# Seven half products for eight in the first SwiGLU too, some low parts by accumulating loads, and one conditioning vector moved to the second SwiGLU

## The chip, the cores and the metric

The kernel runs on one core of one Trainium2 chip. The metric is device time of one execution in microseconds. The kernel before takes 1032.04 us, the median of three runs between 1031.98 and 1033.32 us. Differences of about 0.2%, some 2 us, can be told from no change.

## What is computed

One decoder layer on 512 tokens of width 1024, in float32:

```python
def _swiglu(h, w_gate, w_up, w_down):
    return (jax.nn.silu(h @ w_gate) * (h @ w_up)) @ w_down
...
c_act = jax.nn.silu(c)
mod = (c_act @ w_ada[l] + b_ada[l]).reshape(B, N_MOD, D_MODEL)[:, :, None, :]
sh1, sc1, gt1, sh2, sc2, gt2, sh3, sc3, gt3 = [mod[:, i] for i in range(N_MOD)]
h = _modulate(_rmsnorm(x, g_ffn1[l]), sh1, sc1)
x = x + MACARON_W * gt1 * _swiglu(h, w1_gate[l], w1_up[l], w1_down[l])
h = _modulate(_rmsnorm(x, g_mix[l]), sh2, sc2)
x = x + gt2 * _hybrid_mixer(h, ...)
h = _modulate(_rmsnorm(x, g_ffn2[l]), sh3, sc3)
x = x + MACARON_W * gt3 * _swiglu(h, w2_gate[l], w2_up[l], w2_down[l])
return _rmsnorm(x, g_final)
```

The hidden width of both SwiGLUs is 2816, that is 22 blocks of 128. The mixer between them (a convolution and an attention branch) has the same code before and after. The nine vectors of `mod` condition the three parts; vector 8 is `gt3`, the gate of the second SwiGLU.

## The kernel before

**Precision.** Every float32 operand of a product is split in a high part (rounded to float32r) and a low part (the rest), and a product is three matmuls: high by high, low by high, high by low. For weights, a unit of 128x1024 values is loaded by SP into one of four buffers `raw`; ScalarE copies it to `whi` (L496); VectorE, or now and then GpSimd, subtracts and writes `wlo` (L435, `low_part`). There are four pairs `whi`, `wlo`, so a unit is split three or four units ahead of its use.

**Stages.** The first SwiGLU (`ffn`, from about 60 to 407 us of the trace), the mixer (to about 640 us) and the second SwiGLU (`ffn2`, to the end). In `ffn` each of the blocks 3 to 21 is a pair of full products, gate and up (`project`): 2 x 8 x 2 x 3 = 96 matmuls of 256 columns. The down products come in two halves of 11 blocks (`part`), each added to the residual `x`. While it runs, VectorE also multiplies and sums seven conditioning vectors (`ada_sums`, L1242 and L1245, eight instructions each, with their own loads into three buffers `araw`), and builds the rotary tables.

**Seven for eight.** In `ffn2`, from block `PLAIN` = 7 on, the gate and up products of a block are made of seven half products in place of eight (`seven`): 7 x 4 x 3 = 84 matmuls. For that VectorE builds sums of the activations once (`build_t`: `thi`, `tlo`, L819 to L829), sums of the two weight units for each block (`sums`, L461 to L472) with their own high and low parts (`sum_parts`: `wsh`, `wsl`, L479 and L481), and adds the half products up (`collect`, L901 to L922). Two of these adds are waited for by later products of the same block: the product after L908 adds into its bank, and the one after L914 into another. The down products of `ffn2` come in four groups (`SIZES` = 6, 6, 5, 5).

**What sets the order.** A planner (`Plan`) runs the tasks of the program against cost estimates and writes each engine's instructions in one fixed order. For an elementwise step that VectorE or GpSimd can do, it picks one of them; GpSimd is charged with `W_TAX` on top.

Of the kernel before, what the change touches and what calls it, by code (L numbers as in the profile page):

```python
# [25 lines left out]
FH = FK // 2  # L26
# [4 lines left out]
PLAIN = 7  # L31
# [65 lines left out]
N_AW = 3  # L97
LATER, ADA_FROM = 3, 2
# [17 lines left out]
R_T = 0.9  # L116
# [177 lines left out]
def tile_hymba_layer(ctx: ExitStack, tc: tile.TileContext, xT, pos, cols_d, con_d, wa0, wa1, f1a, f1b, f1d,  # L294
# [62 lines left out]
    def ffn_units(wa, wb, wd):  # L357
        u = [wa[d] for d in range(DK)]
        u += [wb[f - GRP, i] for f in range(GRP, FH) for i in range(2)]
        u += [wd[0, n] for n in range(FH)]  # L360
        u += [wb[f - GRP, i] for f in range(FH, FK) for i in range(2)]
        return u + [wd[1, n] for n in range(FH)]

# [15 lines left out]
    def seven_units(wa, wb, wd, at):  # L379
# [22 lines left out]
    units += seven_units(f2a, f2b, f2d, len(units))  # L402
# [29 lines left out]
    def low_part(u):  # L432
# [4 lines left out]
        if u not in pair_of or u != pair_of[u].u:  # L437
            give(raws, i)
        done(made[u])
# [45 lines left out]
    def make_units():  # L485
        for u in range(len(units)):
# [13 lines left out]
            go(R_W, low_part(u))  # L500
# [209 lines left out]
    def ffn(s, gp, accs, norm, end):  # L710
        ghi = [gp.tile([P, T], F32R, name=f"ghi{k}") for k in range(FH)]
        glo = [gp.tile([P, T], F32R, name=f"glo{k}") for k in range(FH)]
        sg_of = [gp.tile([P, T], F32, name=f"sg{k}") for k in range(2)]
        lag(64, gp)
        for k in range(KEEP[s]):
            whi_of.append(gp.tile([P, UNIT], F32R, name=f"whik{k}"))
            wlo_of.append(gp.tile([P, UNIT], F32R, name=f"wlok{k}"))
            give(kept[s], len(whi_of) - 1)
        sgs, gs = Slots(range(2)), [Slots([k]) for k in range(FH)]
        g_in = [Event() for _ in range(FK)]  # L720
        gate = [mod[:, 3 * s + 2, d:d + 1] for d in range(DK)]
        at = {}

        def glu(f, bg, bu):
            k = yield sgs
            yield c_act(T)
            nc.scalar.activation(sg_of[k], bank_of[bg], AF.Silu)
            give(banks, bg)
            q = yield scr
            yield c_tt(T)  # L730
            nc.vector.tensor_mul(scr_of[q], sg_of[k], bank_of[bu])  # L731
            give(banks, bu)
            give(sgs, k)
            j = yield gs[f % FH]
            yield c_act(T)
            nc.scalar.activation(ghi[j], scr_of[q], AF.Copy)
            yield c_tt(T)
            nc.vector.tensor_sub(glo[j], scr_of[q], ghi[j].bitcast(F32))
            give(scr, q)
            done(g_in[f])  # L740

        def part(half, d, b, ts, keep=False):
            for k in range(FH):
                n = d * FH + k
                if (half, n // 8) not in at:
                    at[half, n // 8] = take_unit()
                u = at[half, n // 8]
                yield made[u]
                yield g_in[half * FH + k]
                yield c_mm3(ts.stop - ts.start)  # L750
                mm3(bank_of[b][:, ts], cols(u, n % 8), (ghi[k][:, ts], glo[k][:, ts]), k == 0, k == FH - 1)
                if n % 8 == 7 and not keep:
                    free_unit(u)
                if half == 0 and d == DK - 1:
                    give(gs[k], k)

        def first_half(d, b):
            yield c_stt(T)
            nc.vector.scalar_tensor_tensor(x[d], bank_of[b], gate[d], x[d], op0=OP.mult, op1=OP.add)
            give(banks, b)  # L760

        def main():
            for f in range(GRP):
                go(R_GLU, glu(f, accs[2 * f], accs[2 * f + 1]))
            for f in range(GRP, FK):
                if f == FH:
                    for d in range(DK):
                        b = yield banks
                        yield from part(0, d, b, FULL)
                        if d == 0:  # L770
                            yield mod_in[3 * s + 2]
                        go(R_X, first_half(d, b))
                bg = yield banks
                yield from project(bg, N_THIRDS if f == GRP else 0)
                bu = yield banks
                yield from project(bu)
                go(R_GLU, glu(f, bg, bu))
            for d in range(DK - 2):
                b = yield banks
                yield from part(1, d, b, FULL)  # L780
                go(R_X, residual(d, b, gate[d], FULL, norm))
# [5 lines left out]
            for n in range(8, FH):  # L787
                free_unit(at[1, n])
# [1508 lines left out]
```

## Time and profile before

| | before |
|---|---|
| median of 3 runs | 1032.04 us |
| the profiled execution | 1032.0 us |
| its span | 1030.2 us |
| TensorE (PE) busy | 1001.6 us, 97% |
| VectorE (DVE) busy | 723.5 us, 70% |
| ScalarE (ACT) busy | 449.6 us, 44% |
| GpSimd (POOL) busy | 82.2 us, 8% |

1.8 us lie around the span. A busy PE is not a PE at its peak, since matmuls are pipelined: one lasts some 277 ns, while the next starts after some 113 ns. So the cost of a matmul is read from a run of many, not from its own duration.

### The profile page before, as it was taken

The numbers are of one execution on the slowest core, as the hardware profiler recorded it, in microseconds if no ns is written. First come the engines' busy times: TensorE is split into PE (matmuls) and PEld (weight loads), VectorE is DVE, ScalarE is ACT, GpSimd is POOL, SyncE is SP. The second block draws the span as 40 slices with busy tenths as digits, with TensorE's granted clock in tenths as the row PEclk, the third lists the DMA queues.
The fourth block names the chain that finished last, engine by engine and source line by source line (L and its number), as shares of the span: only waits on it lengthen the run. The fifth ranks groups of instructions, "written<-read, shape, count | busy, mean of one in ns | idle before, by whom it ended". The sixth has DMA issues, their size and how long they took to land.

```text
span 1030.2 us, 20507 instructions
## 1 busy us (share of the span) xinstructions
PE 1001.6 (97%) x8589; PEld 974.7 (95%) x8589; DVE 723.5 (70%) x1281; ACT 449.6 (44%) x789; POOL 82.2 (8%) x61
## 2 busy tenths in 40 slices
PE   8899999999999999999999999999999999999996
PEld 5899999999999999998889789999999999999996
DVE  3977556655555544589989896676757976877854
ACT  4542322213223232355967985444424533543533
POOL 0300000000000001111111110011100200100100
PEclk8999999999999999999999999999999999999998
DMA  9656554545545530233511002313322342342312
GB/s 332 266 191 243 181 197 181 205 176 193 201 170 203 184 101 29 89 121 119 197 35 39 18 15 79 119 63 123 103 83 83 106 141 83 103 130 76 103 42 82
DMA packets 40733, 134.02 MB, mean 130 GB/s; under 512 B 4704, under 2 KB 8032, under 8 KB 40000
## 3 DMA queue, kind: packets, MB, share of 16 engines
q1 hardware_dynamic: 40640, 132.71, 37.4%
q8 instruction: 67, 1.10, 0.4%
q14 instruction: 26, 0.21, 0.1%
HBM read 130.14 MB, written 2.10 MB: 128 GB/s over the span
## 4 chain that ended last, share of the span: by engine, by line
PE 77%; DVE 17%; ACT 3%; issue 2%; DMA 1%; SPq 0%; POOL 0%; ACTq 0%; DVEq 0%
PE b L323 67%; PE b L876 9%; DVE wlo L435 2%; DVE PT L1797 2%; DVE P L1714 1%; DVE wsl L481 1%; DVE afirst L1113 1%; DVE raw L468 1%; DMA x<-in_xT_dram 1%; DVE q L1478 1%; DVE s L649 1%; ACT whi L496 0%; DVE glo L845 0%; PE b L1786 0%; DVE s L1428 0%
## 5 line engine op out<-in xcount | busy, mean ns | idle before, releaser
L323 PE MATMUL b<-hhi,whi 128*128 128x256 f32 x1352 | 380.3, 281 | 1.3 <-DVE pc L1637 1.3
L323 PE MATMUL b<-hlo,whi 128*128 128x256 f32 x1352 | 376.0, 278 | 1.0 <-DVE hlo L655 0.6
L323 PE MATMUL b<-hhi,wlo 128*128 128x256 f32 x1352 | 375.6, 278 | 0.5 <-POOL wlo L435 0.5
L496 ACT ACTIVATE whi<-raw 128x1024 fp32r<-128x1024 f32 (+3 forms) x174 | 176.1, 1013 | 328.4 <-issue 157.2
L435 DVE TENSOR_TENSOR wlo<-raw,whi 128x1024 fp32r<-128x1024 f32 (+3 forms) x151 | 185.0, 1226 | 130.7 <-ACT whi L496 129.1
L323 PEld LDWEIGHTS b<-hhi,whi 128*128 128x128 f32 x1352 | 255.5, 189 | 5.8 <-issue 3.5
L323 PEld LDWEIGHTS b<-hlo,whi 128*128 128x128 f32 x1352 | 254.9, 189 | 2.0 <-DVE hlo L655 1.0
L323 PEld LDWEIGHTS b<-hhi,wlo 128*128 128x128 f32 x1352 | 254.9, 189 | 0.7 <-POOL wlo L435 0.7
L323 PE MATMUL b<-ghi,whi 128*128 128x256 f32 x640 | 177.4, 277 | 0.0
L323 PE MATMUL b<-glo,whi 128*128 128x256 f32 x640 | 176.7, 276 | 0.0
L323 PE MATMUL b<-ghi,wlo 128*128 128x256 f32 x640 | 176.7, 276 | 0.0
L323 PEld LDWEIGHTS b<-ghi,whi 128*128 128x128 f32 x640 | 120.1, 188 | 1.2 <-issue 1.2
L323 PEld LDWEIGHTS b<-glo,whi 128*128 128x128 f32 x640 | 120.2, 188 | 0.0
L323 PEld LDWEIGHTS b<-ghi,wlo 128*128 128x128 f32 x640 | 120.1, 188 | 0.0
L435 POOL TENSOR_TENSOR wlo<-raw,whi 128x1024 fp32r<-128x1024 f32 (+2 forms) x23 | 55.6, 2419 | 193.6 <-ACT whi L496 178.1
L1245 DVE SCALAR_TENSOR_TENSOR ada<-araw,cact,ada 128x1024 f32<-128x1024 f32 x49 | 62.7, 1279 | 3.6 <-DMA araw<-in_wa_dram 3.6
L731 DVE TENSOR_TENSOR s<-sg,b 128x512 f32<-128x512 f32 x22 | 15.0, 687 | 38.0 <-PE b L323 38.0
L580 ACT ACTIVATE s<-x 128x256 f32<-128x256 f32 (+1 forms) x41 | 19.4, 492 | 44.6 <-DVE x L662 41.3
L662 DVE SCALAR_TENSOR_TENSOR x<-b,mod,x 128x512 f32<-128x512 f32 (+1 forms) x30 | 18.9, 643 | 28.0 <-PE b L323 28.0
L876 PE MATMUL b<-thi,whi 128*128 128x256 f32 x120 | 33.8, 282 | 1.4 <-DVE s L908 1.4
L876 PE MATMUL b<-tlo,whi 128*128 128x256 f32 x120 | 33.2, 276 | 0.0
L876 PE MATMUL b<-thi,wlo 128*128 128x256 f32 x120 | 33.1, 276 | 0.0
(299 smaller groups left out, 1772.2 us busy)
## 6 DMA issues: line engine op xcount, KB each, us to landing
araw<-in_wa_dram SPq DMA_DIRECT2D x56, 512.0 KB
raw<-in_f1b_dram SPq DMA_DIRECT2D x38, 512.0 KB
raw<-in_f2b_dram SPq DMA_DIRECT2D x38, 512.0 KB
raw<-in_f1d_dram SPq DMA_DIRECT2D x22, 512.0 KB
raw<-in_f2d_dram SPq DMA_DIRECT2D x22, 512.0 KB
raw<-in_wib_dram SPq DMA_DIRECT2D x14, 512.0 KB
wfirst<-in_wa_dram SPq DMA_DIRECT2D x5, 1024.0 KB
raw<-in_wc_dram SPq DMA_DIRECT2D x8, 512.0 KB
```

The source lines that it names most:

```text
L323: nc.tensor.matmul(o, lhsT, rhs, start=start, stop=stop)
L435: (nc.vector if e == DVE else nc.gpsimd).tensor_sub(wlo_of[j][:, :n], raw_of[i][:, :n], whi_of[j][:, :n].bitcast(F32))
L468: either(e).tensor_sub(ga[:, E], s1, ga[:, E])
L481: either(e).tensor_sub(lo, v, hi.bitcast(F32))
L496: nc.scalar.activation(whi_of[j][:, :n], raw_of[raw_at[u]][:, :n], AF.Copy)
L580: nc.scalar.activation(o[:, ts], x[d][:, ts], AF.Square)
L649: nc.vector.scalar_tensor_tensor(t, x[d][:, ts], am[:, s, d:d + 1], rb(), op0=OP.mult, op1=OP.mult)
L662: nc.vector.scalar_tensor_tensor(x[d][:, ts], bank_of[b][:, ts], gate, x[d][:, ts], op0=OP.mult, op1=OP.add)
L731: nc.vector.tensor_mul(scr_of[q], sg_of[k], bank_of[bu])
L876: nc.tensor.matmul(o, u, v, start=start and not e and not i, stop=e == DK // 2 - 1 and i == 2, skip_group_check=not start)
L1245: nc.vector.scalar_tensor_tensor(a, w, cact[:, k:k + 1], a, op0=OP.mult, op1=OP.add)
L1797: nc.vector.tensor_sub(pl[:, :w], pt[:, :w], ph[:, :w].bitcast(F32))
```

## The change

1. `ffn` and `ffn2` become one function. The first SwiGLU takes the second's form: four groups of down products, and for the blocks from 11 on (`PLAIN[0]` = 11, eleven pairs) seven half products. In the second, `PLAIN[2]` = 6 in place of 7: one pair more.
2. `low_by_load`: for every second unit of the down weights from the third of a group on, in groups whose end is past `PLAIN` and without the last two units of all, the low part is made otherwise. ScalarE writes minus the rounded weights to `wlo`, and a load issued by GpSimd adds the weights to it. These are 5 units in the first SwiGLU and 7 in the second.
3. The buffers of the conditioning vectors are two in place of three, and one sum in place of two; they live as long as the kernel. Their loads are tied to other weight loads (`ada_after`), and the eight of vector 8 come in the second SwiGLU.

The core of the diff:

```diff
-PLAIN = 7
+PLAIN = {0: 11, 2: 6}
...
-N_AW = 3
-LATER, ADA_FROM = 3, 2
+N_AW = 2
+ADA_LATE = 3.0
...
-R_T = 0.9
+R_T = {0: 3.5, 2: 0.9}
...
+    by_load = set()
+
+    def ffn_units(s, wa, wb, wd, at):
         u = [wa[d] for d in range(DK)]
         for what, n in _steps():
             if what == "d":
+                if GROUP[n + 1] >= PLAIN[s]:
+                    by_load.update(range(at + len(u) + 2, at + len(u) + SIZES[n], 2))
                 u += [wd[i] for i in range(GROUP[n], GROUP[n + 1])]
                 continue
-            if n >= PLAIN:
+            if n >= PLAIN[s]:
                 pair_of[at + len(u)] = pair_of[at + len(u) + 1] = Pair(at + len(u))
             u += [wb[n - GRP, i] for i in range(2)]
+        by_load.difference_update(range(at + len(u) - 2, at + len(u)))
         return u
 
-    units = ffn_units(f1a, f1b, f1d)
+    units = ffn_units(0, f1a, f1b, f1d, 0)
...
+    def low_by_load(u):
+
+        n, i, j = units[u].shape[-1], raw_at[u], w_at[u]
+        yield c_act(n)
+        nc.scalar.activation(wlo_of[j][:, :n], raw_of[i][:, :n], AF.Copy, scale=-1.0)
+        give(raws, i)
+        yield POOL, 0.9
+        nc.gpsimd.dma_start(wlo_of[j][:, :n], units[u], accum_op=OP.add)
+        yield DMA, 0.73 * 4 * n * 1e-3
         done(made[u])
...
-            go(R_W, low_part(u))
+            go(R_W, (low_by_load if u in by_load else low_part)(u))
...
+    def ada_after(n):
+
+        if n >= 6 * DK:
+            return n_mix + DK + (n - 6 * DK) // 2
+        return DK + 2 + (n if n < 30 else 30 + (n - 30) * 2) * 4 // 5
...
-        plan.run(mod_in[8])
+        plan.run(mod_in[6])
```

What this does to the order is shown at three places. In the names, a number behind `_` tells one buffer from another.

On VectorE in the first SwiGLU, after the first down products: before, the work of two plain blocks (L731 and L738 are one block's product with its gate and its low part) and sums of a conditioning vector:

```order
L1242 TENSOR_SCALAR ada_769<-araw_768,cact 128x1024
L731 TENSOR_TENSOR s_75<-sg_797,b_70 128x512
L435 TENSOR_TENSOR wlo_94<-raw_89,whi_93 128x1024
L738 TENSOR_TENSOR glo_785<-s_75,ghi_774 128x512
L1245 SCALAR_TENSOR_TENSOR ada_769<-araw_766,cact,ada_769 128x1024
```

And now, at the first block of seven half products (L831 to L848 are the adds of `collect`, L490 the low parts of weight sums, L433 the old L435, L1175 the old L1245):

```order
L831 TENSOR_TENSOR s_74<-s_74,b_70 128x256
L1175 SCALAR_TENSOR_TENSOR ada<-araw_764,cact,ada 128x1024
L834 TENSOR_TENSOR s_74<-s_74,b_70 128x256
L490 TENSOR_TENSOR wsl_793<-raw_89,wsh_792 128x512
L840 TENSOR_TENSOR s_75<-s_74,b_64 128x256
L490 TENSOR_TENSOR wsl_793<-raw_89,wsh_792 128x512
L433 TENSOR_TENSOR wlo_98<-raw_92,whi_97 128x1024
L844 TENSOR_TENSOR s_75<-s_74,b_70 128x256
L433 TENSOR_TENSOR wlo_100<-raw_91,whi_99 128x1024
L848 TENSOR_TENSOR b_64<-s_74,b_64 128x256
```

L834 and L840, which the matmuls of the same block wait for, now stand in one queue with the conditioning sums; between L834 and the matmul that waits for it stand 5 to 19 other matmuls in the eleven blocks, and 11 to 13 behind L840. In the second SwiGLU before, these two leads are 5 to 19 (L908) and 9 to 11 (L914).

On VectorE at the end of the first SwiGLU: the last residual of the first half of the tokens, the inverse root (`v`), and the first operands of the mixer (`hlo`). Before:

```order
L662 SCALAR_TENSOR_TENSOR x<-b_70,mod,x 128x256
L613 TENSOR_SCALAR v_80<-b_65 128x2
L519 TENSOR_SCALAR v_80<-v_80 128x2
L523 SCALAR_TENSOR_TENSOR v_80<-v_80 128x2
L525 TENSOR_TENSOR v_80<-v_80 128x2
L527 SCALAR_TENSOR_TENSOR v_80<-v_80 128x2
L529 SCALAR_TENSOR_TENSOR v_80<-v_80 128x2
L531 SCALAR_TENSOR_TENSOR v_80<-v_80 128x2
L533 TENSOR_TENSOR v_80<-v_80 128x2
L535 SCALAR_TENSOR_TENSOR v_80<-v_80 128x2
L662 SCALAR_TENSOR_TENSOR x<-b_66,mod,x 128x256
L649 SCALAR_TENSOR_TENSOR s_75<-x,am,b_65 128x256
```

Now, from the same residual's last small step on:

```order
L542 TENSOR_TENSOR v_80<-v_80 128x2
L544 SCALAR_TENSOR_TENSOR v_80<-v_80 128x2
L671 SCALAR_TENSOR_TENSOR x<-b_64,mod,x 128x256
L658 SCALAR_TENSOR_TENSOR s_75<-x,am,b_63 128x256
L658 SCALAR_TENSOR_TENSOR s_76<-x,am,b_63 128x256
L658 SCALAR_TENSOR_TENSOR s_73<-x,am,b_63 128x256
L622 TENSOR_SCALAR v_81<-b_66 128x2
L664 SCALAR_TENSOR_TENSOR hlo_113<-s_75,mod,hhi_105 128x256
```

The residual that stands between the inverse root and the first operands is now the very last of the SwiGLU. On TensorE, 2 x 33 matmuls of the second half of the tokens stood behind the end of the first half; now it is 2 x 15, since the last group has 5 blocks for 11.

On GpSimd, before, nothing stood between the start and the clearing of the mixer's buffers:

```order
L1105 TENSOR_TENSOR afirst_133<-afirst_133 128x256 x2
L1381 MEMSET swp_4247 128x512
```

Now the low parts of some units and the accumulating loads stand there (the last of them here):

```order
L433 TENSOR_TENSOR wlo_96<-raw_90,whi_95 128x1024
L446 DMA wlo_94<-in_f1d_dram 128x1024
L446 DMA wlo_98<-in_f1d_dram 128x1024
L490 TENSOR_TENSOR wsl_795<-s_75,wsh_794 128x512
L433 TENSOR_TENSOR wlo_94<-raw_90,whi_93 128x1024
L433 TENSOR_TENSOR wlo_98<-raw_89,whi_97 128x1024
L446 DMA wlo_96<-in_f1d_dram 128x1024
L1310 MEMSET swp_4311 128x512
```

Between an accumulating load and the first matmul that waits for it stand 105 matmuls (seven of the twelve) or 129 (five). In all, TensorE has 144 matmuls less, twelve for each of the twelve new pairs. Behind the mixer's first products, its instructions stand on all engines as before.

## Rows read from the trace of the kernel before

**Rows 1.** The page: busy time of each engine, with its share of the span

```profile
PE 1001.6 (97%) x8589; PEld 974.7 (95%) x8589; DVE 723.5 (70%) x1281; ACT 449.6 (44%) x789; POOL 82.2 (8%) x61
```

**Rows 2.** Stretches: length, busy time by engine, granted clock, DMA share, GB/s

```profile
100.00:140.00 40.00, 40.00 (x349) 39.46 (x348) 22.06 (x24) 11.23 (x15) 0.00 (x0) 1.00 0.52 185
180.00:220.00 40.00, 40.00 (x357) 39.46 (x356) 26.38 (x31) 8.95 (x10) 0.00 (x0) 1.00 0.51 186
260.00:300.00 40.00, 40.00 (x356) 39.46 (x355) 20.64 (x22) 11.34 (x15) 0.00 (x0) 1.00 0.56 210
...
800.00:840.00 40.00, 39.01 (x340) 38.56 (x340) 36.76 (x56) 20.26 (x30) 7.91 (x3) 1.00 0.42 132
840.00:880.00 40.00, 40.00 (x356) 40.00 (x355) 26.36 (x36) 13.26 (x16) 0.00 (x0) 1.00 0.29 87
880.00:920.00 40.00, 39.54 (x348) 39.28 (x347) 36.48 (x56) 20.87 (x30) 6.83 (x3) 1.00 0.37 125
```

**Rows 3.** What PE waited for, 60 to 415 us: total, times, longest

```profile
PE b L622 <- DVE v L535: 0.6, 1, 0.6
PE b L323 <- DVE afirst L1116: 0.2, 1, 0.2
```

**Rows 4.** What PE waited for, 640 us to the end

```profile
PE b L876 <- DVE s L908: 1.4, 3, 0.5
```

**Rows 5.** The chain that ended last: start, length, matmuls in a row

```profile
116.23 45.96 PE b L323 x392
...
252.20 44.33 PE b L323 x392
...
783.90 13.61 PE b L876 x120
```

**Rows 6.** Groups by form: count, busy us, mean ns, idle before

```profile
L435 DVE TENSOR_TENSOR wlo<-raw,whi 128x1024 fp32r<-128x1024 f32 x125 | 158.9, 1272 | 103.4 <-ACT whi L496 101.8 <-PE b L323 0.8 <-DMA araw<-in_wa_dram 0.6
L1245 DVE SCALAR_TENSOR_TENSOR ada<-araw,cact,ada 128x1024 f32<-128x1024 f32 x49 | 62.7, 1279 | 3.6 <-DMA araw<-in_wa_dram 3.6
L481 DVE TENSOR_TENSOR wsl<-raw,wsh 128x512 fp32r<-128x512 f32 x30 | 19.8, 682 | 0.1
L980 DVE SCALAR_TENSOR_TENSOR x<-b,mod,x 128x512 f32<-128x512 f32 x24 | 18.0, 749 | 10.6 <-PE b L323 10.3
L905 DVE TENSOR_TENSOR s<-s,b 128x256 f32<-128x256 f32 x15 | 6.2, 416 | 8.7 <-PE b L876 8.7
```

**Rows 7.** VectorE in order of time, in a dense stretch: start, length

```profile
802.41 1.22 DVE L435 TENSOR_TENSOR wlo<-raw,whi 128x1024 fp32r<-128x1024 f32 x1
803.55 0.42 DVE L922 TENSOR_TENSOR b<-s,b 128x256 f32<-128x256 f32 x1
...
812.50 3.31 DVE L435 TENSOR_TENSOR wlo<-raw,whi 128x1024 fp32r<-128x1024 f32 x1
```

**Rows 8.** GpSimd in the same stretch

```profile
802.79 3.10 POOL L435 TENSOR_TENSOR wlo<-raw,whi 128x1024 fp32r<-128x1024 f32 x1 [5.14 <-ACT whi L496]
812.32 2.41 POOL L435 TENSOR_TENSOR wlo<-raw,whi 128x1024 fp32r<-128x1024 f32 x1 [6.42 <-ACT whi L496]
```

**Rows 9.** VectorE in order of time: end of the first SwiGLU, end of the second

```profile
398.67 0.48 DVE L662 SCALAR_TENSOR_TENSOR x<-b,mod,x 128x256 f32<-128x256 f32 x1 [2.85 <-PE b L323]
...
404.63 1.27 DVE L649 SCALAR_TENSOR_TENSOR s<-x,am,b 128x256 f32<-128x256 f32 x3 [1.15 <-PE b L622]
405.81 1.27 DVE L655 SCALAR_TENSOR_TENSOR hlo<-s,mod,hhi 128x256 fp32r<-128x256 f32 x3
...
1013.12 0.48 DVE L662 SCALAR_TENSOR_TENSOR x<-b,mod,x 128x256 f32<-128x256 f32 x1 [0.86 <-PE b L323]
...
1017.51 0.16 DVE L535 SCALAR_TENSOR_TENSOR v<-v 128x2 f32<-128x2 f32 x1
```

**Rows 10.** TensorE in order of time: transposes, then the mixer's first two matmuls

```profile
404.21 0.38 PE L622 MATMUL b<-con,v 128*128 128x128 f32 x2
...
406.91 0.28 PE L323 MATMUL b<-hhi,whi 128*128 128x256 f32 x1
407.03 0.28 PE L323 MATMUL b<-hlo,whi 128*128 128x256 f32 x1
```

**Rows 11.** Two loads on SP's queue

```profile
259.42 0.33 SPq L424 DMA_DIRECT2D raw<-in_f1b_dram  x1
259.80 0.50 SPq L1228 DMA_DIRECT2D araw<-in_wa_dram  x1
```

**Rows 12.** The VectorE step that waited for the second of these loads

```profile
263.95 1.28 DVE L1245 SCALAR_TENSOR_TENSOR ada<-araw,cact,ada 128x1024 f32<-128x1024 f32 x1 [0.59 <-DMA araw<-in_wa_dram]
```

More of the change, by code (lines that the diff above doesn't have):

```diff
@@ L354, in tile_hymba_layer @@
     ident = kv("ident")
[L357 to L362, printed above, removed]
     pair_of = {}
@@ L438, in low_part @@
             give(raws, i)
+        done(made[u])
+    def low_by_load(u):
[6 more added lines that the diff above has]
+        yield DMA, 0.73 * 4 * n * 1e-3
         done(made[u])
@@ L710, in ffn @@
     def ffn(s, gp, accs, norm, end):
[L711 to L781, printed above, removed]
-            for ts in HALVES:
-                for d in (DK - 2, DK - 1):
-                    b = yield banks
-                    yield from part(1, d, b, ts, True)
-                    go(R_X, residual(d, b, gate[d], ts, norm))
-            for n in range(8, FH):
-                free_unit(at[1, n])
-            done(end)
@@ L791, in ffn @@
-        go(R_MAIN, main())
-    def ffn2(s, gp, accs, norm, end):
         ghi = [gp.tile([P, T], F32R, name=f"ghi{k}") for k in range(max(SIZES))]
@@ L985, in keep @@
                 yield halves_
-            for hi, lo in half_of:
+            for hi, lo in mine:
                 whi_of.append(hi)
@@ L995, in main @@
             for what, n in _steps():
-                if what == "f" and n >= PLAIN:
+                if what == "f" and n >= PLAIN[s]:
                     yield from seven(n)
@@ L1035, in ffn2 @@
         for e in range(DK // 2):
-            go(R_T, build_t(e))
+            go(R_T[s], build_t(e))
         go(R_MAIN, main())
@@ L1213, in tile_hymba_layer @@
     stab = const.tile([P, T], F32, name="stab")
-    aside = ExitStack()
-    aq = aside.enter_context(tc.tile_pool(name="aq", bufs=1))
-    aw = [aq.tile([P, D], F32, name=f"araw{i}") for i in range(N_AW)]
-    ada = [aq.tile([P, D], F32, name=f"ada{i}") for i in range(2)]
-    aws, adas = Slots(range(N_AW)), Slots(range(2))
+    aw = [const.tile([P, D], F32, name=f"araw{i}") for i in range(N_AW)]
+    ada = const.tile([P, D], F32, name="ada")
+    aws, adas = Slots(range(N_AW)), Slots([0])
     aw_in = [Event() for _ in range(7 * DK)]
@@ L1225, in ada_loads @@
             i = yield aws
-            yield loaded[DK + ADA_FROM + n]
+            yield loaded[ada_after(n)]
             yield c_dma(4 * D)
@@ L1237, in ada_sums, with ada_reduce @@
             if k == 0:
-                j = yield adas
-            a, w = ada[j], aw[aw_at[n]]
+                yield adas
+            w = aw[aw_at[n]]
             if k == 0:
                 yield c_ts(D)
-                nc.vector.tensor_scalar(a, w, cact[:, 0:1], None, op0=OP.mult)
+                nc.vector.tensor_scalar(ada, w, cact[:, 0:1], None, op0=OP.mult)
             else:
                 yield c_stt(D)
-                nc.vector.scalar_tensor_tensor(a, w, cact[:, k:k + 1], a, op0=OP.mult, op1=OP.add)
+                nc.vector.scalar_tensor_tensor(ada, w, cact[:, k:k + 1], ada, op0=OP.mult, op1=OP.add)
             give(aws, aw_at[n])
             if k == DK - 1:
-                summed.append((order[i], j))
-            if summed and k == LATER:
-                go(R_ADA, ada_reduce(*summed.pop()))
-        yield made[n_ffn - 1]
-        go(R_ADA, ada_reduce(*summed.pop()))
-    def ada_reduce(m, j):
+                soon = Event()
+                soon.done = (plan.at[0] + ADA_LATE, DVE)
+                go(R_ADA, ada_reduce(order[i], soon))
+    def ada_reduce(m, soon):
+        yield soon
         b = yield banks
@@ L2152, in tile_hymba_layer @@
         squared = norm.squared
-        ffn2(2, gp, accs, norm, end)
+        ffn(2, gp, accs, norm, end)
         for d in range(DK):
```

26 lines of the change are left out of this document (8 added, 18 removed).

## The prediction

> **What bounds the kernel now.** I read the page's busy times first, then the stretches, then what TensorE waited for. PE is busy for 97% of the span [rows 1], and in the first SwiGLU for all of it: the stretches from 100, 180 and 260 us show 40.00 of 40 us, with VectorE at 21 to 26 [rows 2]. There PE waits for 0.8 us in all, none of it inside the blocks [rows 3]. So PE's own count of matmuls sets that stage, and a matmul taken away there comes back as time, as long as VectorE follows. In the second SwiGLU, which already has fifteen blocks of seven half products, PE waits too, but little: three times, 1.4 us in all, for the add of L908 [rows 4]. Where: the stretches from 800 and 880 us, with VectorE at 36.8 and 36.5 of 40 us, lost 0.99 and 0.46 us of PE; the one from 840 us, with VectorE at 26.4, lost none [rows 2]. That is the pattern to reason with: PE is free of losses up to some 75% of VectorE and loses 1 to 2.5% above 90%.
>
> **The matmuls taken away.** Twelve pairs lose 12 matmuls each: 144. The price of one is the pace of a long run: 44.33 us for 392, so 0.1131 us, and 13.61 us for 120 of the seven half products, so 0.1134 [rows 5]. With 0.1132 this is 144 x 0.1132 = **-16.3 us**, 14.9 of it in the first SwiGLU. One row warns: from 116 us on, 392 matmuls took 45.96 us, 0.1172 each [rows 5], at a granted clock of 1.00 [rows 2]. I can't tell what starts or ends that pace; such a stretch costs 392 x 0.004 = 1.6 us, and one more or one less of it goes into the range.
>
> **VectorE in the first SwiGLU.** Added for each of eleven pairs: four sums of 512 and three low parts of 512 at 0.68 us (L481's row stands for all two-input steps of that width) and five adds of 256 at 0.416 [rows 6], so 7 x 0.68 + 5 x 0.416 = 6.8 us, times 11 = 75 us. The sums of activations, once: 16 x 0.68 + 16 x 0.416 = 17.5. Two more groups of down products are added to x: 16 x 0.749 = 12. Gone: vector 8, seven sums of 1.28 and a first step that I put at half of one, 9.6; five subtractions of 1.27 that become loads, 6.4 [rows 6]. Together some +89 us. The three stretches shown hold 69.1 us in 120, or 58% [rows 2]; over about 320 us this is 184. Now 273 in about 305 us: 90%. Half of the conditioning sums stand ahead of the first seven-product block, which flattens it, but all eleven blocks run with VectorE as loaded as in the two dense stretches of the second SwiGLU.
>
> What VectorE delays is PE through the adds L834 and L840, with leads of 5 to 19 matmuls, or 0.6 to 2.1 us. One conditioning sum (1.28) or one blocked step in front is enough. Behind a late add stand PE's next products, and nothing else overtakes on PE. The price: the two dense stretches hold about four such blocks each and lost 0.25 and 0.12 us a block. Ends: nothing at all, or for each of 22 adds the longest wait seen, 0.5 [rows 4], 11 us. I take the higher of the two measured prices, since these stretches are the nearest in kind: 11 x 0.23 = **+2.5 us**.
>
> GpSimd makes it a little worse. It gets about ten of the weight subtractions. While it ran one for 2.41 us from 812.32 on, VectorE's own subtraction took 3.31 us in place of 1.22 [rows 7, 8]. So handing over 1.2 us of work held VectorE for 2.1. This is in the dense stretches' price already.
>
> **The accumulating loads.** ScalarE takes 1 us each more, five in the first stage; it is busy for under 12 of 40 us there [rows 2], so nothing. The trace has no accumulating load. The nearest rows are two plain loads issued at 259.42 and 259.80 us, of which the second had landed by 263.95 [rows 11, 12]: 4.2 us for 1 MB. The cover is 105 matmuls x 0.1132 = 11.9 us, or 14.6 for the five with 129. One end: it lands like a plain load, and the wait is nothing. Other end: it moves the bytes three times (read, read, write), 3 x 4.2 = 12.6, plus a microsecond of queueing on GpSimd: 1.7 us late, seven times, 12 us. I take nothing, for the rows hold two loads in 4.2 us and one load alone must be shorter. Below nothing is excluded: PE does not wait for these parts today. Only a page has a price for a load of this kind: the Trainium skill, "DMA: Bandwidth & Descriptors", section "Anatomy of one DMA — SWDGE (gpsimd) path", gives 2.0 us plus bytes over 436 GB/s for a load issued by GpSimd, without accumulating, which by my estimate is 3.2 us for 512 KB and leaves the sum as it is; no run here shows it yet.
>
> **The end of the first SwiGLU.** This is what the diff does not tell. The first half of the tokens ends with a residual, and then come its square, the inverse root, transposes, and the mixer's first operands, before PE can start the mixer. Before, PE has 66 matmuls of the second half to do meanwhile: residual at 398.67, first mixer matmuls at 406.91 and 407.03, no gap [rows 9, 10]. Now it has 30, at 0.118 (the spacing of these last rows) 3.5 us, plus three pairs of small sums, about 1.2: 4.7. The chain: from the residual to the end of the inverse root 4.55 us, as at the end of the second SwiGLU, which has the same short blocks (1013.12 to 1017.67) [rows 9]; transposes to first product 0.4, that to the high part about 0.5, high part to low part 1.1 [rows 9, 10]: 6.6. PE stands for 6.6 - 4.7 = 1.9 us: **+2.0 us**. Ends: 0.5, if the steps overlap better, and 3.5, if the second half's inverse root gets in front of the second operand.
>
> **The second SwiGLU.** One block of seven more and vector 8 (10 us of VectorE) near its start, where build_t also runs and GpSimd gets five steps; three or four more blocks in dense company x 0.23 = **+0.8 us** (ends 0 and 2). Seven fewer subtractions relieve the rest. The loads of vector 8 cost nothing: the DMA engines are at 0.29 to 0.42 there [rows 2]. With two buffers for three, the conditioning loads stand closer to their use; they are SP's, and the next weight loads stand behind them in its queue, covered by the same 12 us.
>
> **Sum.** -16.3 + 2.5 + 2.0 + 0.8 = -11.0 us. The profiled execution took 1032.0 us, the median 1032.04: **1021.0 us**.
>
> **Rivals.**
> VectorE becomes the bound. For it: 90% is an average, and the first stage has conditioning sums of 1.28 us between the adds, which the second never had. Against it: VectorE's steps start 0.08 us before the end of the one in front (802.41 + 1.22 is 803.63, the next starts at 803.55 [rows 7]), so the real load is nearer 82%, and a backlog is worked off in the down products. With 0.6 us a block in place of 0.23 on 27 blocks it is 1021 + 10 = 1031 at worst; about 1026 to 1028 in the middle.
>
> All is hidden: no waits beyond today's, and a transition of 0.5 us: 1032.0 - 16.3 + 0.5 = 1016, or 1014.6 if the slow stretch goes as well.
>
> Slower: the accumulating loads land late. The mechanism is that GpSimd must write out such a load itself, and that VectorE holds it off while it runs two-input steps without a gap. For it: one step can hold the other engine out [rows 7, 8]. Against it: GpSimd's subtraction at 802.79, begun while VectorE ran without a gap, took 3.10 us and not 2.41 [rows 7, 8], a delay of 0.7. It decides from a landing of 12 us on; at 13.5 us, 7 x 1.6 = 11 us eat the gain, and at 16 us, 7 x 4.1 + 5 x 1.4 = 36 us make 1057. The Trainium skill, "SBUF — State Buffer", section "SBUF: two separate sides", has this as a trap: VectorE in a two-port mode keeps GpSimd from writing descriptors, and the load only seems slow. By that rule two-input steps hold off only what reads the buffer, so the trap would need other steps than this stage mostly has; the held-off rows agree with its lock, and no run here shows the trap.
>
> That the change does not do what it says is excluded for the count of matmuls, which the order shows.
>
> **How the numbers follow.** Forecast 0.63 (1018 to 1024); VectorE as the bound 0.19 (1024 to 1031, a quarter of it within 0.2%, which is about what can be told from no change); all hidden 0.12; loads late 0.06. The range of 1015 to 1027.5 holds the forecast, nearly all of the hidden case and more than a third of the bound one: 0.82. Faster: 0.63 + 0.12 + 0.15 = 0.90. Same: 0.05. Slower: 0.05.
>
> **What would show it.** PE at 0.113 per matmul in the blocks of the first SwiGLU; short waits on L834 and L840, of a fraction of a microsecond, 2 to 3 us in all; a gap of about 2 us where the mixer's first matmuls stand; no wait on the accumulating loads. Wrong would be a wait of PE on a low part made by a load, PE under 95% busy over the eleven blocks, or a mixer of another length.

## The result, and the profile after

The changed kernel took 1024.94 us (median of 8, 1022.24 to 1029.51), the kernel before 1033.11 beside it (1031.98 to 1035.84): a ratio of 0.9917, 95% interval 0.9896 to 0.9937. It is faster, by 8.2 us where 11.0 were forecast. Its profiled execution took 1028.29 us, with a span of 1026.4.

The page, busy time of each engine, which answers to [rows 1]:

```profile
PE 993.0 (97%) x8445; PEld 965.3 (94%) x8445; DVE 811.5 (79%) x1443; ACT 492.3 (48%) x857; POOL 138.3 (13%) x91
```

The 144 matmuls are gone (8589 to 8445), but PE's busy time fell by 8.6 us and not by 16.3. Stretches of the changed kernel, columns as in [rows 2]:

```profile
60.00:400.00 340.00, 337.02 (x2924) 332.14 (x2923) 278.30 (x390) 133.05 (x188) 46.26 (x28) 1.00 0.54 180
260.00:300.00 40.00, 38.54 (x335) 37.48 (x334) 36.53 (x59) 19.73 (x29) 9.54 (x4) 1.00 0.49 180
300.00:340.00 40.00, 40.00 (x342) 40.00 (x342) 33.20 (x43) 15.08 (x20) 6.36 (x3) 1.00 0.53 164
840.00:880.00 40.00, 40.00 (x356) 40.00 (x355) 26.20 (x38) 14.89 (x18) 0.87 (x1) 1.00 0.42 113
```

VectorE is busy for 278.3 of 340 us in the first SwiGLU (82%), and for 36.5 of 40 in its fullest stretch. What stands out is the third line: PE is busy for all of 40 us, at a granted clock of 1.00, and does 342 matmuls; in the fourth, as busy, it does 356. What PE waited for, 58 to 400 us, and then 640 to 1010 (total, times, longest; [rows 3, 4] before):

```profile
PE b L802 <- DVE s L834: 1.7, 3, 0.8
PE b L323 <- ACT s L589: 0.8, 1, 0.8
PE b L323 <- DVE hlo L664: 0.4, 1, 0.4
...
PE b L323 <- DVE ada L1175: 2.1, 1, 2.1
PE b L802 <- DVE s L834: 1.4, 3, 0.5
PE b L1198 <- ACT s L1195: 0.4, 1, 0.4
```

The waits on L834 are there and small. None is on an accumulating load. The 2.1 us for L1175 is new: it is the sum of vector 8, now in the second SwiGLU. TensorE in order of time around the wait on L834 at 295 us (start, length):

```profile
295.05 0.28 PE L802 MATMUL b<-hhi,whi 128*128 128x256 f32 x1
295.17 0.28 PE L802 MATMUL b<-hlo,whi 128*128 128x256 f32 x1
295.28 0.28 PE L802 MATMUL b<-hhi,wlo 128*128 128x256 f32 x1
295.49 0.38 PE L802 MATMUL b<-thi,whi 128*128 128x256 f32 x1
295.71 0.28 PE L802 MATMUL b<-tlo,whi 128*128 128x256 f32 x1
295.82 0.28 PE L802 MATMUL b<-thi,wlo 128*128 128x256 f32 x1
295.94 0.28 PE L802 MATMUL b<-thi,whi 128*128 128x256 f32 x1
296.06 0.28 PE L802 MATMUL b<-tlo,whi 128*128 128x256 f32 x1
296.18 0.28 PE L802 MATMUL b<-thi,wlo 128*128 128x256 f32 x1
```

The interruption itself is 0.2 us. Ahead of it the starts are 0.1133 us apart on average, behind it 0.1178, and that lasts until 342 us, where the sum of a conditioning vector interrupts PE again. This is the slow stretch that the prediction saw once (from 116 us on, [rows 5]) and gave 1.6 us. In the two SwiGLUs of this trace 224 us run at the slow pace. A us of it does 0.0044 / 0.1178 = 3.7% less, so 8.4 us are lost there; the profiled execution of before held 56 us, 2.1. (Here and below the mixer's first products, up to some 440 us, are counted with the SwiGLUs.)

### The profile page after: what moved, and what is told of

Read it like the earlier page. It is cut to its first block, busy times and chain, and to the rows that moved or that the text cites. A ratio compares the mean times of both kernels' runs of the same rounds, so it can differ in the third digit from the quotient of the medians.

```text
span 1026.4 us, 20544 instructions
## 1 busy us (share of the span) xinstructions
PE 993.0 (97%) x8445; PEld 965.3 (94%) x8445; DVE 811.5 (79%) x1443; ACT 492.3 (48%) x857; POOL 138.3 (13%) x91
## 4 chain that ended last, share of the span: by engine, by line
PE 74%; DVE 19%; ACT 2%; issue 2%; DMA 1%; SPq 0%; ACTq 0%; DVEq 0%
PE b L323 54%; PE b L802 19%; DVE wlo L433 3%; DVE PT L1726 1%; DVE glo L771 1%; DVE wsl L490 1%; DVE s L749 1%; DVE raw L477 1%; DVE tlo L755 1%; PE b L1715 1%; DVE afirst L1039 1%; DVE ada L1175 1%; DVE P L1643 1%; DMA x<-in_xT_dram 1%; DVE s L658 1%
## 5 line engine op out<-in xcount | busy, mean ns | idle before, releaser
L323 PE MATMUL b<-hhi,whi 128*128 128x256 f32 (+1 forms) x968 | 274.4, 283 | 1.3 <-DVE pc L1566 1.3
L323 PE MATMUL b<-hlo,whi 128*128 128x256 f32 (+1 forms) x968 | 270.3, 279 | 1.4 <-DVE hlo L664 1.0
L323 PE MATMUL b<-hhi,wlo 128*128 128x256 f32 (+1 forms) x968 | 269.6, 279 | 0.0
L433 DVE TENSOR_TENSOR wlo<-raw,whi 128x1024 fp32r<-128x1024 f32 (+3 forms) x131 | 159.3, 1218 | 42.9 <-ACT whi L505 42.6
L323 PEld LDWEIGHTS b<-hhi,whi 128*128 128x128 f32 x968 | 182.8, 189 | 5.4 <-issue 3.1
L323 PEld LDWEIGHTS b<-hlo,whi 128*128 128x128 f32 x968 | 183.3, 189 | 2.6 <-DVE hlo L664 1.6
L323 PEld LDWEIGHTS b<-hhi,wlo 128*128 128x128 f32 x968 | 183.2, 189 | 0.0
L433 POOL TENSOR_TENSOR wlo<-raw,whi 128x1024 fp32r<-128x1024 f32 (+2 forms) x31 | 88.1, 2843 | 374.1 <-ACT whi L505 342.1
L1175 DVE SCALAR_TENSOR_TENSOR ada<-araw,cact,ada 128x1024 f32<-128x1024 f32 x49 | 66.7, 1361 | 24.3 <-DMA araw<-in_wa_dram 24.3
L802 PE MATMUL b<-hhi,whi 128*128 128x256 f32 x216 | 60.2, 279 | 0.0
L802 PE MATMUL b<-thi,wsh 128*128 128x256 f32 x216 | 60.0, 278 | 0.0
L802 PE MATMUL b<-hhi,wlo 128*128 128x256 f32 x216 | 59.9, 277 | 0.0
```

Source lines behind the costliest of these rows:

```text
L323: nc.tensor.matmul(o, lhsT, rhs, start=start, stop=stop)
L433: (nc.vector if e == DVE else nc.gpsimd).tensor_sub(wlo_of[j][:, :n], raw_of[i][:, :n], whi_of[j][:, :n].bitcast(F32))
L802: nc.tensor.matmul(o, u, v, start=start and not e and not i, stop=e == DK // 2 - 1 and i == 2, skip_group_check=not start)
L1175: nc.vector.scalar_tensor_tensor(ada, w, cact[:, k:k + 1], ada, op0=OP.mult, op1=OP.add)
```

## The experiments: is it the pace?

The theory (A): PE runs each stretch between two interruptions at one of two paces, and which one falls anew at each interruption; apart from this, and from falls of the clock shown below, the change brought what was summed. The rival (B): waits for VectorE, the transition or the loads ate the difference.

**The same kernels again.** No edit.

> The changed kernel once more, nothing altered, for a second trace. Theory A (two paces): TensorE runs each stretch between two interruptions either at 0.1133 us or at 0.1177 us per 256-column matmul, both at a granted clock of 1.00, and which one it is falls anew at every interruption. In the first trace of this kernel some 220 us ran at the slow pace, which cost 220 x 0.0044 / 0.1177 = 8 us of its 1028.3. So a second trace has other slow stretches, and its time is 1020 us plus 0.037 us for each us of slow stretch, within 1.5 us. Theory B (VectorE): the spread comes from the length of TensorE's waits for VectorE; then the slow stretches stand at the same places in both traces, and the time follows the waits (7 us of them in the blocks of the first trace of the two SwiGLUs).

It took 1025.77 us, with 138 us of slow stretches, most of them at 74 to 112, 115 to 138, 288 to 297 and 667 to 727 us; the first trace had them at 113 to 136, 296 to 342, 355 to 394, 669 to 728 and 906 to 964. Of the waits, L834's came to 1.6 and 1.4 us, as before. So it is not the waits that move. Theory A had 1020 + 5.1 = 1025.1 us. Two of the five places are slow in both traces, though: where it happens is not wholly left to chance.

> The changed kernel unaltered, timed on the same chip as the two below. By the pace theory its profiled time is 1019 us plus 0.037 us for each us of the two SwiGLUs that ran at 0.1177 us a matmul plus 1.7 us for each stretch of 3 to 4 us behind a wait in which the granted clock was 0.5: 1018 to 1021 once both are taken off, as 1019.5 and 1018.4 in the first two traces.

(The two that it speaks of are the kernel with fifteen tiny matmuls and the attempt at a better kernel, further down.) The median of six was 1026.87, the ratio 0.991 (0.9879 to 0.9942). The profiled one took 1031.52 with 244 us of slow stretches, 32 of them in the mixer's first products. In both repeats a second thing shows: the granted clock falls behind a gap on PE. Stretches of the second trace, then of the third, columns as above:

```profile
726.00:730.00 4.00, 2.02 (x21) 1.43 (x19) 4.00 (x7) 4.00 (x8) 0.00 (x0) 1.00 0.00 0
730.00:734.00 4.00, 4.00 (x21) 4.00 (x22) 4.00 (x7) 2.03 (x4) 0.00 (x0) 0.57 0.06 14
734.00:738.00 4.00, 4.00 (x38) 4.00 (x37) 3.56 (x6) 1.86 (x3) 0.00 (x0) 1.00 0.92 311
```

```profile
398.00:402.00 4.00, 2.85 (x16) 2.32 (x17) 3.51 (x15) 1.70 (x4) 2.99 (x7) 0.87 0.02 6
402.00:404.00 2.00, 2.00 (x12) 2.00 (x10) 1.51 (x6) 0.39 (x1) 1.35 (x6) 0.50 0.00 0
```

PE stands for 2 us for vector 8, or for 1.2 where the mixer starts, and then runs for 3 to 4 us at 0.50 of its clock, which is 1.2 GHz: 1.7 us lost each time (in one trace further down, with a wait of 3.6 us, the fall is twice as long). It is not certain to happen: behind the wait for vector 8 in 6 of 9 traces in which that wait was 1.9 to 3.6 us, behind the start of the mixer in 8 of the 11 that have the changed kernel's ending.

> The kernel before, unaltered, for a second trace of it. Taking off 0.0374 us for each us of the two SwiGLUs at 0.1177 us a matmul, and what stretches with a granted clock of 0.5 behind a wait lost, three traces of the changed kernel leave 1019.9, 1018.9 and 1019.0 us, and the one trace of the kernel before leaves 1029.9. Theory A (the work saved and its waits come to 10.6 us as summed, and the rest of the difference between two executions is pace and clock): a second trace leaves 1029 to 1031 us whatever its own time is. Theory B (pace and clock do not account for the spread of a kernel): it leaves something else by more than 1.5 us.

The kernel before took 1039.27 us in this trace, 7.3 more than in its first, with 270 us of slow stretches in place of 56. The same piece of the program (712 to 798 us, the undivided and the first halved blocks of the second SwiGLU), in the first trace and in this one:

```profile
712.00:798.00 86.00, 86.00 (x761) 86.00 (x760) 58.85 (x80) 34.42 (x48) 10.15 (x4) 1.00 0.30 93
```

```profile
712.00:798.00 86.00, 86.00 (x732) 86.00 (x732) 57.12 (x77) 31.96 (x44) 8.53 (x3) 1.00 0.29 88
```

Same program, same busy time, same clock, 29 matmuls fewer. Taking pace and clock off:

| trace | time | slow pace | clock | left |
|---|---|---|---|---|
| before | 1032.00 | 2.1 | 0 | 1029.9 |
| before, again | 1039.27 | 10.1 | 0 | 1029.2 |
| after | 1028.29 | 8.4 | 0 | 1019.9 |
| after, again | 1025.77 | 5.2 | 1.7 | 1018.9 |
| after, third | 1031.52 | 9.1 | 3.4 | 1019.0 |

Executions of one kernel that lie 6 or 7 us apart come to within 1 us of each other. The change is worth 1029.6 - 1019.3 = 10.3 us.

**What sets the pace.** In all 14 traces I cut the SwiGLUs at every interruption of PE and took the mean spacing of each piece of at least 12 full matmuls: 421 pieces, of which 331 have 0.113 to 0.1145 us, 89 have 0.1165 to 0.118, and one lies between. So a change of pace inside a piece is as good as absent. But an interruption is no independent draw: with pieces cut in this way, in the twelve traces without extra matmuls the next piece of the same SwiGLU is slow in 31 of 68 cases behind a slow one and in 33 of 212 behind a fast one. That the pace "falls anew at every interruption" is more than the traces show; what went before, or the place in the program, weighs too. Three kernels test what can be done to the pace.

```
 in part(), g < 3, ahead of each column block:
+    mm(bank_of[b][:, 0:1], ident, kv("one"), True, True)
```

> The changed kernel with one extra matmul (128x128 weights, one column, into a bank that the next product overwrites) ahead of each of the 24 column blocks of the first three groups' output in both SwiGLUs: 48 interruptions of TensorE of 0.1 to 0.2 us that wait for nothing. Theory A: each interruption throws the pace anew, so that the stretches between are a mix of 0.1133 and 0.1177 us a matmul, with borders at the extra matmuls and hardly elsewhere. Theory B: the pace is set by what VectorE or the loads do beside TensorE, and the borders stand where they stood. The time itself: 5 to 10 us for the interruptions.

It took 1040.25 us. Behind 47 of the 48 extra matmuls the pace was the fast one (behind one it could not be read). Neither theory said so: A expected a mix, and B borders that stay where they were. Most of the 47 follow a piece that was fast already; at three of them (115, 751 and 928 us) the piece ahead was slow, and there the pace changed. One of them in order of time, with 0.1178 us a matmul ahead of it and 0.1134 behind:

```profile
751.01 0.28 PE L323 MATMUL b<-con 128*128 128x1 f32 x2
751.15 0.37 PE L323 MATMUL b<-ghi,whi 128*128 128x256 f32 x1
751.35 0.28 PE L323 MATMUL b<-glo,whi 128*128 128x256 f32 x1
```

The five slow pieces that were left begin behind a wait for VectorE (289, 740, 915 and 974 us) or behind the transposes of a conditioning vector (113). My price for it was too low: 0.23 us for each, 11 in all, and 5 us of clock behind longer waits.

```
 in ada_reduce(), behind the transposes; in project(), where n_thirds > 0;
 in part(), at the head of a group's first column block:
+    mm(bank_of[b][:, 0:2], z[:, :P], z[:, 0:2], True, True)   # z: ident read as 16 bit
```

> The changed kernel with a tiny extra matmul (128x128 weights, two columns, 16 bit, into a bank that is overwritten) in some 17 places: behind the sum of each conditioning vector, ahead of the first undivided block of each SwiGLU, and at the head of the outputs of each of its groups but the last. In the kernel with 48 extra matmuls the stretch behind 47 of them ran at 0.1133 us a matmul, and each took 0.23 us. Theory A (an interruption that waits for nothing lets the pace fall back to the fast one): the slow stretches of the two SwiGLUs come to 15 to 60 us instead of 50 to 230, and the time is that of the changed kernel plus 17 x 0.1 to 0.23 us less 2 to 4 us: from 2 us less to 2 us more, with a narrower spread. Theory B (those 47 were chance): slow stretches as before, and 2 to 4 us more.

With such a matmul in fifteen places, 55 us of slow pace remained (31 of them in the mixer's first products), but what is left without pace and clock rose to 1022.0, 0.18 us for each place. At the two places where the piece ahead was slow (298 and 744 us) it was fast behind. The time was 1025.65 (1021.46 to 1028.48) beside 1026.87 (ratio to before 0.9902, 0.9873 to 0.9932): no difference, and the spread is no narrower. The 55 us are what theory A gave, but one trace does not decide it: two kernels below without such a matmul (the first and the third of the next section) held 24 and 53 us. As a cure it saves nothing that shows.

```
 in mm3() and product():
-    w[0] x0, w[0] x1, w[1] x0
+    w[0] x0, w[1] x0, w[0] x1
```

> The changed kernel with the three matmuls of every exact product in another order: high weights by high input, low weights by high input, high weights by low input (the last two change places), everywhere that the shared helper and the halved pairs issue them; the same count. In the slow stretches of the traces every third weight load is 0.192 instead of 0.188 us and the matmul behind it starts 0.013 us late. Theory A: the slow pace hangs on the order of the three (the same weights are loaded twice running); then it is gone in this kernel, its profile has under 20 us of it, and the time is 3 to 6 us lower. Theory B: the pace is a matter of how the stream is entered after an interruption, whatever the order: slow stretches are there as before, 50 to 250 us in all, and the time is within 2 us.

141 us of slow pace, 31 of them in the mixer's first products, and 1027.63 us (ratio 0.992, 0.9892 to 0.9947). The order of the three is not the cause; A of this run's expectation is wrong. What in the timing of an interruption decides the pace stays open.

## The experiments: the terms of the sum

**No halved pair in the first SwiGLU.**

```
-PLAIN = {0: 11, 2: 6}
+PLAIN = {0: 99, 2: 6}        # and no build_t in the first
```

> The changed kernel with no halved pair in the first SwiGLU (all its pairs in eight half products, no accumulating load there); the rest of the change stays: groups of 6, 6, 5, 5 in the first SwiGLU, the last conditioning vector late, 16 halved pairs in the second. By the sum of the prediction the eleven pairs give 11 x 12 matmuls x 0.1132 = 14.9 us less 2.5 us of waits, so this kernel takes 12.4 us more than the changed one: 1037 us beside 1025. If TensorE's waits and its slow pace in the first SwiGLU are brought by the halved pairs, the pairs are worth less, and it takes 7 to 11 us more: 1032 to 1036. If the pairs were bound by VectorE it would be under 6 us.

1036.15 us (ratio 1.0015, 0.9994 to 1.0035): without these pairs nothing is left of the gain. In time it is 9.3 to 11.2 us, by the two medians of the changed kernel; its trace leaves 1031.8 without pace and clock, 12.5 more than the changed kernel's 1019.3, where the sum said 12.4. It had one slow stretch of 24 us and none behind L834 in the first SwiGLU, since there is no L834 there. That the pairs are bound by VectorE is out.

**No accumulating loads.**

```
-                if GROUP[n + 1] >= PLAIN[s]:
+                if False:
```

> The changed kernel with every low part of the weights by a subtraction, none by an accumulating load. Theory A: the loads only take work from VectorE that has room anyway, so the time stays within 1.5 us (0.15%), and TensorE's waits for VectorE in the first SwiGLU grow by less than 1 us. Theory B (VectorE is at its limit there): 12 subtractions of 1.2 us come back, those of them in the first SwiGLU reach TensorE, and the time grows by 3 to 6 us.

1027.09 us (ratio 0.9932, 0.9905 to 0.9959), 1018.1 without pace and clock (1.2 less than the changed kernel, whose own traces differ by 1.0), with 1.3 us of waits on L834 in the first SwiGLU for 1.7. Theory A: the loads neither cost nor bring anything that shows.

**The last vector's sum later.**

```
-                soon.done = (plan.at[0] + ADA_LATE, DVE)
+                soon.done = (plan.at[0] + (ADA_LATE if i < 6 else 8.0), DVE)
```

> The changed kernel with the sum over partitions of the last conditioning vector put 5 us later in TensorE's order (42 matmuls further behind the vector's last step on VectorE). In the trace of the changed kernel TensorE waits 2.1 us there for VectorE and 0.4 us for the copy behind it. Theory: both waits go, and the time falls by 2 to 2.5 us; the rival is that VectorE's lateness shows at the next wait instead, and under 0.7 us is left.

What PE waited for between 640 and 1005 us in this kernel:

```profile
PE b L802 <- DVE wsl L490: 1.1, 1, 1.1
PE b L802 <- DVE s L834: 1.0, 2, 0.5
PE b L1198 <- ACT s L1195: 0.7, 1, 0.7
```

The 2.1 us are gone, and 1.1 us on another of VectorE's steps and 0.7 for the copy stand in their place: of 2.5 us 1.8 are left. The rival was right: VectorE is full there (10.00 of 10 us in each of the three stretches from 700 to 730), and whoever asks next waits. 1026.09 us, ratio 0.9912 (0.9882 to 0.9942); its trace leaves 1020.7 without pace and clock, no better than the changed kernel's 1019.3.

**A longer cover at the end of the first SwiGLU.**

```
-            for d in range(3, DK - 2): ...   # then two halves of the last 2
+            for d in range(3, DK - 4): ...   # then two halves of the last 4, first SwiGLU alone
```

> The changed kernel with the last four column blocks of the first SwiGLU's output in two halves of the positions, not the last two, so that 60 matmuls instead of 30 stand on TensorE between the end of the first half and the start of the mixer. In three traces of the changed kernel and its neighbours TensorE idles there between 393 and 402 us: waits of 0.8 and 0.4 us and small matmuls between, and in three of five traces the granted clock falls to 0.5 for 3 to 4 us right behind it. Theory: the short cover costs 1.5 to 2 us, and 1.7 more where the clock falls; this kernel is 1.5 to 3.5 us faster. Rival: the second half's chain is what ends last and has no cover in either, so under 0.7 us changes.

The stretch from 390 to 416 us in the kernel before, in the changed one and in this one:

```profile
390.00:416.00 26.00, 25.44 (x220) 25.24 (x219) 15.31 (x43) 6.88 (x15) 6.39 (x13) 1.00 0.10 31
```

```profile
390.00:416.00 26.00, 24.85 (x213) 24.32 (x213) 20.44 (x59) 10.92 (x23) 4.35 (x12) 1.00 0.11 32
```

```profile
390.00:416.00 26.00, 24.30 (x206) 23.73 (x205) 20.91 (x53) 12.03 (x24) 6.10 (x13) 1.00 0.16 50
```

PE stands for 0.56, 1.15 and 1.70 us. (In the kernel before this window ends earlier in the program; the account at the end compares like with like.) More cover for the first half of the positions made it worse, for then PE waits 1.3 us for the inverse root of the second half (L544), at 404 us, whose cover is the mixer's work on the first. The time was the same, 0.9914 (0.9882 to 0.9945). The rival was right.

**Nothing of the SwiGLUs' additions on GpSimd.**

```
-W_TAX = 4
+W_TAX = 400
```

> The changed kernel with none of the SwiGLUs' and weights' additions and subtractions on GpSimd, all on VectorE (the planner's surcharge for GpSimd is set out of reach; the start and the mixer's own work on it keep theirs). In the trace of the changed kernel VectorE's instructions that run beside one on GpSimd take 2.1 to 2.8 us instead of 0.68, and two of TensorE's waits of 0.5 us and more for the addition to the third product stand right behind such a one. Theory A: GpSimd's share holds VectorE up, so these waits shrink and the time falls by 0 to 2 us. Theory B: VectorE needs the relief; with some 20 us more work at its fullest places TensorE waits 3 us or more longer, and the time grows by 2 to 5 us.

1042.46 us, 1.0057 (1.0037 to 1.0076) of the kernel before. What PE waited for between 60 and 110 us, and between 640 and 1000:

```profile
PE b L323 <- DVE wlo L433: 6.6, 1, 6.6
...
PE b L323 <- DVE wlo L433: 7.6, 1, 7.6
PE b L802 <- DVE wsl L490: 1.2, 3, 0.4
PE b L802 <- DVE s L834: 0.3, 1, 0.3
```

Theory B, by more than I gave it. But not where I looked: the two large waits stand at the head of each SwiGLU, where build_t runs, and in the halved blocks the waits on L834 are smaller than with GpSimd's help (0.3 us in the second SwiGLU for 1.4), while 1.2 us on L490 stand there that the changed kernel doesn't have: in sum no less. In the first SwiGLU it is the same, 1.3 us on L490 in place of 1.7 on L834. The clock falls behind both large ones, 0.91 on average from 60 to 100 us.

**An attempt at a better kernel.** The low part of each pair's first weights by an accumulating load, and the last vector four units earlier.

```
                 pair_of[...] = Pair(at + len(u))
+                by_load.add(at + len(u))
...                               # and the sums wait for ScalarE's read of the unit, not for its low part
...
-            return n_mix + DK + (n - 6 * DK) // 2
+            return n_mix + DK + (n - 6 * DK - 4) // 2
```

> The changed kernel with two edits that take work from VectorE where TensorE waits for it: the low part of the first weights of each halved pair is made by an accumulating load too (27 subtractions of 1.2 us less on VectorE, or of 3 us less on GpSimd, where they hold VectorE's own up), and the last conditioning vector is loaded four units earlier, so that its last step lies ahead of the full stretch of VectorE. Theory A (VectorE's lateness inside the blocks makes the waits, and the waits let the slow pace in): TensorE's waits for the third product fall from 3.1 us in both SwiGLUs to under 1, the 2.1 us wait for the last vector goes, and the time falls by 3 to 7 us, to 1018 to 1022. Theory B: the loads, 27 more of 0.5 MB on top of the 12, land late or hold up the plain loads, and the time is the same or up to 5 us longer.

The waits did what A says: L834 0.4 us in both SwiGLUs together, none for vector 8's L1175. The time did not: 1028.69 us (0.993, 0.9902 to 0.9958). Its profiled execution had 235 us of slow pace, 106 of it behind L834 at 896, 906 and 974 us, where no wait long enough to be listed is left but PE is still interrupted for 0.1 us; and 2.9 us of new waits (1.5 for a weight's low part, 1.4 for an operand) stand where the second SwiGLU begins, beside the earlier vector, with a fall of the clock behind them. Without pace and clock 1018.4 is left, 0.9 us less than the changed kernel. None of these kernels is faster than it by more than the noise.

## Why the prediction was right, and where it was not

The time lay in the range, on the side of the rival of a bound VectorE, but not for its reason. That the 10.3 us without pace and clock come so near to the 11.0 of the sum is in part luck: the transition cost 2 us less than reckoned, and the waits of vector 8's sum on PE close to 3 us that were not in it. The stages, each without pace and clock (cut at the first and last product that reads ghi in each SwiGLU):

| stage | before, 2 traces | after, 3 traces | difference |
|---|---|---|---|
| first SwiGLU, from 58 us | 346.9, 346.6 | 334.6, 334.3, 334.6 | -12.2 |
| to the second's first output | 344.1, 344.2 | 346.4, 345.6, 345.3 | +1.6 |
| the second's outputs | 266.5, 266.0 | 266.4, 266.5, 266.5 | +0.2 |

- **The matmuls.** Right in count and price: 0.1133 us in the fast pieces.
- **VectorE in the first SwiGLU, +2.5.** About right. The stage gave 12.2 for the 12.4 summed. It flatters a little: vector 8's own sum on PE, 1.0 us by the starts around such a sum, left this stage for the next, so the waits and restarts cost 3.7 beside the kernel before. Beside the kernel without halved pairs there, whose stage left 346.5, the pairs gave 12.0, and their waits cost 2.9; the five interruptions on L834 in the first trace come to the same 2.9 by the starts. L834 was the place, at 0.8 us at the longest; L840 never was. (The price of 0.25 a block that the prediction works out is used there as 0.23; 0.25 would have made 2.7.)
- **VectorE's load.** 82% over the stage and 91% at the fullest, where 90% was reckoned and 82% allowed for. The rival of a bound VectorE was met by some of the times and, in the halved blocks, not by its mechanism: 2.9 us on eleven blocks are 0.26 us a block, not 0.6. Nor does its share of busy time decide: from 700 to 720 us of the first trace VectorE is busy throughout and PE loses nothing; from 720 to 730, where PE asks for vector 8, it loses 1.4 us.
- **The accumulating loads, 0.** Right, and the cover was not too long: issue to landing took 8.5 us in the first SwiGLU and 6.5 in the second (medians; the longest of the twelve took 9.3), by the list of DMA issues:

```profile
wlo<-in_f2d_dram POOLq DMA_DIRECT2D x7, 512.0 KB, 6.5
wlo<-in_f1d_dram POOLq DMA_DIRECT2D x5, 512.0 KB, 8.5
```

  That is inside the 11.9 us. The 4.2 us of two plain loads (4.5 from the issue of the first) were no guide to it. The Trainium skill, "DMA: Bandwidth & Descriptors", section "Anatomy of one DMA — SWDGE (gpsimd) path", came to an estimated 3.2 us for a load that doesn't add; the measurement of one that does is 2 to 2.7 times that.
- **The end of the first SwiGLU, +2.0.** Too much: beside the kernel before it came to nothing. The gap itself is there and near its size: by the starts PE loses 0.9 us to the square of the second half (L589), which stands in front of the mixer's first product, and 0.7 to L664, 1.6 where 1.9 were reckoned. But "no gap" before was read from the first half of the tokens alone. A little later PE waited there too, 0.7 us by the starts for the second half's inverse root at 414 us and 0.7 for a weight's low part from GpSimd at 422. The waits of before from 404 to 430 us:

```profile
PE b L622 <- DVE v L535: 0.6, 1, 0.6
PE b L323 <- POOL wlo L435: 0.5, 1, 0.5
```

  Neither is left in the changed kernel, and the 22 us from the last output product on hold as much work in the kernel before as in the changed one:

```profile
406.80:428.80 22.00, 20.96 (x181) 20.56 (x180) 17.35 (x40) 9.04 (x18) 8.24 (x14) 1.00 0.17 58
```

```profile
396.60:418.60 22.00, 20.85 (x180) 20.32 (x179) 17.33 (x46) 10.39 (x20) 4.35 (x12) 1.00 0.13 40
```

  What the step also left out is that the gap can bring the clock down behind it, 1.7 us more, which it does in most traces.
- **The second SwiGLU, +0.8.** The blocks cost 0.2. But vector 8 was reckoned as VectorE's work alone; its sum on PE waits 2.1 + 0.4 us, and the clock may fall behind that too. The stage between shows +1.6 on average and +2.2 in the first trace, where the clock held: -1.4 for the sixteenth pair's twelve matmuls, +1.0 for the moved sum, +2.8 for its waits by the starts and nothing for the transition make 2.4. The two traces in which the clock fell there leave 1.5 and 1.2; why they leave less stays open.
- **The pace, 1.6 either way.** This is the term that failed in size. One stretch more or less was allowed; the traces hold 5 to 9 us of it after and 2 to 10 before. The forecast was made from an execution of the kernel before with little of it. At that one's 2.1 us the changed kernel would take 1019.3 + 2.1 = 1021.4 us, beside the forecast of 1021.0. Over all executions the medians are 1034.6 us (77, 1030.6 to 1041.4) and 1025.8 (15, 1022.2 to 1031.5), 8.8 us apart: of the 10.3 us that the change is worth, 1.5 is lost on the way. The falls of the clock can be that (three in the three traces of after, none in the two of before), but five traces are too few to divide it between them and the pace.

## What to carry to other kernels

A kernel bound by TensorE whose executions differ by 1% needs a second trace before its terms are summed: the count of matmuls in a stretch of equal length and equal clock shows at once whether one of them ran at the other pace. A wait of 0.2 us in TensorE's stream can be worth more than 0.2 us, since the pace can change there for the 40 us behind it, and one of 2 us can cost 1.7 more by the clock. When a new gap is priced, look for the waits of before that it replaces, also a little behind the place. When a reduction is moved to where another engine has room, look also at the one that must consume its result, and at what that engine's queue holds at that moment.

## What the runs showed of the hardware that was not expected

- Two paces of TensorE at a granted clock of 1.00: 0.1133 and 0.1178 us for 256 columns, held from one interruption to the next (89 of 421 pieces slow), and not drawn independently at each. In the slow one, one weight load in three lasts 0.192 us and not 0.188. The Trainium skill, "TensorE: Matmul & The Clock Gate", section "Wait — 56ns, not 53.3ns?", gives one pace, columns over 2.4 GHz and about 2.5 ns, an estimated 0.109 us here. The 16-bit matmuls of zeros at the start of the changed kernel's trace agree (0.109 us from 5.97 to 6.74 us, at 1.00); no run of wide float32 products in any trace ran at it (0.1133 at the least).
- An extra matmul that waits for nothing was followed by the fast pace 47 times of 48, at 0.23 us; three of the 47 stood behind a slow piece.
- Behind waits of 1.2 to 3.6 us the granted clock went down to 0.50 in 14 of 20 cases, at 1.7 us each (3.4 in one).
- A load that adds to what is in SBUF took 5.7 to 8.8 us from issue to landing for 512 KB (medians of 5 to 16 loads).
